# Shift and scale of an adaLN layer by fp32 products with the weight blocks as stationary operand

## The chip, the cores and the metric

The kernel runs on one core of a Trainium2 chip. TensorE (PE) multiplies, VectorE (DVE), ScalarE (ACT) and GpSimd (POOL) do the element-wise work, SyncE (SP) issues most DMAs. The metric is the device time of one execution in microseconds (us), as the median of several runs. A trace of one execution, taken by the hardware profiler, gives the times of single instructions; "PEld" in it is TensorE's weight load, which is recorded apart from the matmul.

## The reference

One layer of a hybrid decoder: a prompt of 4096 tokens and eight sample tokens, with 1024 features. What matters here is its beginning:

```python
mod = (c @ w_ada + b_ada)[:, None, :]          # c: (1, 1024) and (8, 1024), w_ada: (1024, 3072)
shift, scale, gate = jnp.split(mod, 3, axis=-1)
h = x * (1 + scale) + shift
proj = h @ w_in
...
y = layer_norm(DEEPNORM_ALPHA * x + (1 + gate) * mix, ln_g, ln_b)
```

`c` has nine rows in all, one for the prompt and eight for the samples. Nothing of the projection can start before shift and scale are there. Everything behind `proj` (a gated delta rule in chunks with a recurrent state, sliding-window attention, output projection, normalisation) is the same before and after the change.

## The kernel before

The kernel keeps features on the partitions: `shiftT`, `scaleT` and `gateT` are tiles of 128 partitions x 8 blocks x 9 rows of `c`. Phase 1 (`body`, up to line 736) runs over 16 stretches of 256 tokens: `xt` scales and shifts x into `hT`, an fp16 high part and an fp16 low part, and `front` multiplies it by 12 weight blocks `w1` of 128 columns, each split into fp16 high and low parts, with 24 products of 256 columns per block (`group`, line 307), beside 32 small products for `bd` (lines 265 and 267). Then come the recurrent parts of the stretch (`gdn_inv`, `gdn_c`) and side work: `gate_cols` and `dec_a` in the first stretches, preparation of later weights (`prep`, `prep_s`). Phases 2 and 3 follow with attention, the z gates and the output.

The stage that the change touches lies ahead of all this. w_ada's first 2048 columns are read in 16 pieces of 512 KB (`ada`, line 147: 128 rows of 1024 columns, in the order of the rows), each into one of six buffers that `raw` hands out in turn (three names, two buffers each). ACT casts a piece to fp16 (`split`, line 178), DVE forms the low part (line 179), and PE multiplies the pieces as moving operand, 512 columns at a time, with the 18 columns of `cT16` (c's high and low part) as stationary operand (line 190). The results are rows: they are copied out of PSUM (lines 195 and 197), turned by 16 fp32 products with two stacked identities (line 200), and b_ada is added (`shiftT` line 201, `scaleT` line 202).

Right behind it, `xt(0, xs, True)` (line 700) forms hT of the first stretch in four pairs of blocks: ACT and DVE scale and shift one block each (lines 253 and 250), ACT casts the pair (line 255), DVE forms the low part (line 256). `hs32` and `hsT` are the same for the samples (lines 206 to 209). The w1 blocks are fetched through the same six buffers (`fetch_w1`, line 216) and split by ACT and DVE (`split_w1`), first blocks 4 to 7, then the others.

`gate_cols` (line 164), which runs one block for each stretch as side work, already uses the other form: blocks of w_ada as stationary fp32 operand, `cT` as moving operand of 9 columns (line 173).

A scheduler orders the instructions of each engine when the program is built; on the chip every engine, and SP's queue of DMAs, works through its own list in order. A buffer is written again only when its readers are done, and dependencies are kept by the region of a tile that an instruction touches (PE reads the high part of hT's first pair before the others are written).

Of the kernel before, what the change touches and what calls it, by code (L numbers as in the profile page):

```python
# [9 lines left out]
F32 = mybir.dt.float32  # L10
F16 = mybir.dt.float16
BF16 = mybir.dt.bfloat16
AF = mybir.ActivationFunctionType
ALU = mybir.AluOpType
# [9 lines left out]
IWS = 1.0 / WS  # L24
# [9 lines left out]
def body(ctx, tc, I, O, seq):  # L34
# [3 lines left out]
    pe, act, dve, pool, sp = nc.tensor, nc.scalar, nc.vector, nc.gpsimd, nc.sync  # L38

    def mm(out, l, r, st=True, sp_=True):  # L40
        pe.matmul(out, l, r, start=st, stop=sp_)  # L41
# [5 lines left out]
    cf = cst.tile([128, 713], F32, name="cf")  # L47
# [25 lines left out]
    shiftT = cst.tile([128, 8, 9], F32, name="shiftT")  # L73
    scaleT = cst.tile([128, 8, 9], F32, name="scaleT")
    gateT = cst.tile([128, 8, 9], F32, name="gateT")
    cols = cst.tile([128, 73], F32, name="cols")
# [34 lines left out]
    with ExitStack() as p1:  # L111
# [3 lines left out]
        w1p = p1.enter_context(tc.tile_pool(name="w1p", bufs=1))  # L115
        stg = p1.enter_context(tc.tile_pool(name="stg", bufs=2))
        wk = p1.enter_context(tc.tile_pool(name="wk", bufs=2))
        sml = p1.enter_context(tc.tile_pool(name="sml", bufs=2))
        pga = p1.enter_context(tc.tile_pool(name="pga", bufs=1, space=PSUM))
# [3 lines left out]
        pgi = p1.enter_context(tc.tile_pool(name="pgi", bufs=3, space=PSUM))  # L123
# [4 lines left out]
        def xt_ps(shape, dt=F32):  # L128
            return pxt.tile(shape, dt, name="xt")

        def load_x(s):

            xs = []
            for q in range(2):
                x = wf.tile([128, 4, 256], F32, name="x", bufs=3)
                sp.dma_start(x, I["xT"][s][:, 4 * q:4 * q + 4])
                xs.append(x)
            return xs
# [3 lines left out]
        def raw():  # L142

            nraw[0] += 1
            return wk.tile([128, 1024], F32, name=("Aqk", "Kd", "Vn")[nraw[0] % 3], bufs=2)

        def ada(i):
            st = raw()
            sp.dma_start(st, I["w_ada"][0, i // 2 * 128:i // 2 * 128 + 128, i % 2 * 1024:i % 2 * 1024 + 1024])
            return st  # L150

        adas = [ada(i) for i in range(6)]
        cT = w1p.tile([128, 8, 9], F32, name="cT")
        act.dma_start(cT, I["cT"])
        act.dma_start(cols, I["cols"])
        hs32 = w1p.tile([128, 8, 8], F32, name="hs32")
        act.dma_start(hs32, I["xsT"])
        xs = load_x(0)
        cT16 = w1p.tile([128, 8, 18], F16, name="cT16")
        dve.tensor_copy(cT16[:, :, 0:9], cT)  # L160
        dve.tensor_sub(cT16[:, :, 9:18], cT, cT16[:, :, 0:9])
        dve.tensor_scalar(cw64, cols[:, 60:72], IWS, None, op0=ALU.mult)

        def gate_cols():
            part, dst, one = 2, gateT, 1.0
            for blk in range(8):
                cc = part * 8 + blk
                ps = xt_ps([128, 9])
                for hf in range(2):
                    st = stg.tile([128, 4, 256], F32, name="stg")[:, 0:2].rearrange("p a (b c) -> p (a b) c", c=128)  # L170
                    sp.dma_start(st, I["wg"][blk][:, 4 * hf:4 * hf + 4])
                    for k in range(4):
                        mm(ps, st[:, k, :], cT[:, 4 * hf + k, :], hf + k == 0, hf + k == 4)
                dve.tensor_scalar(dst[:, blk, :], ps, cols[:, cc:cc + 1], one, op0=ALU.add, op1=ALU.add)
                yield

        def split(dst_h, dst_l, src):
            act.activation(dst_h, src, AF.Copy, scale=WS)
            dve.scalar_tensor_tensor(dst_l, src, WS, dst_h, op0=ALU.mult, op1=ALU.subtract)


        rps = [pgi.tile([18, 512], F32, name="pgi") for _ in range(3)] + [pga.tile([18, 512], F32, name="pga")]
        for k in range(8):
            w16 = wk.tile([128, 2, 2, 1024], F16, name="kqv", bufs=2)
            for z in range(2):
                st = adas[2 * k + z] if 2 * k + z < 6 else ada(2 * k + z)
                split(w16[:, z, 0], w16[:, z, 1], st)
                for wi, m in ((0, 18), (1, 9)):
                    for q in range(2):
                        mm(rps[2 * z + q][0:m], cT16[:, k, 0:m], w16[:, z, wi, q * 512:(q + 1) * 512],  # L190
                           k + wi == 0, k == 7 and wi == 1)
        arow = wk.tile([18, 2048], F32, name="kqv", bufs=2)
        for q in range(4):
            if q % 2 == 0:
                act.activation(arow[:, q * 512:(q + 1) * 512], rps[q], AF.Copy, scale=IWS)
            else:
                dve.tensor_scalar(arow[:, q * 512:(q + 1) * 512], rps[q], IWS, None, op0=ALU.mult)
        ps = pgi.tile([128, 16, 9], F32, name="pgi")
        for b in range(16):
            mm(ps[:, b, :], arow[:, b * 128:(b + 1) * 128], cf[0:18, 704:713])  # L200
        dve.tensor_add(shiftT, ps[:, 0:8, :], cols[:, 0:8, None].to_broadcast([128, 8, 9]))
        dve.scalar_tensor_tensor(scaleT, ps[:, 8:16, :], 1.0, cols[:, 8:16, None].to_broadcast([128, 8, 9]),
                                 op0=ALU.add, op1=ALU.add)


        dve.tensor_mul(hs32, hs32, scaleT[:, :, 1:9])
# [497 lines left out]
        for g in (0, 1, 2, 3, 8, 9, 10, 11):  # L704
            split_w1(g, fetch_w1(g))
        npre = npres = 0
        sides = [gate_cols(), dec_a()]

        def ahead(s):
            if s < NS:  # L710
                nxt[0] = xt(s, load_x(s))

        for s in range(NS):
            kqv, G, sc, U16, Aqk, Kd, Vn, eGl, vt, vt16 = front(s, nxt[0], lambda: ahead(s + 1))
# [25 lines left out]
    with ExitStack() as p2:  # L740
# [11 lines left out]
        wa = p2a.enter_context(tc.tile_pool(name="wa", bufs=2, **W2))  # L752
        wk = p2a.enter_context(tc.tile_pool(name="wk2", bufs=2, **W2))
# [400 lines left out]
        def mixes(s):  # L1154

            z = zq.pop(s)
            m = []
            for t, (oa, ob) in enumerate(oq_.pop(s)):
                for h in range(4):
                    hs = slice(h * 128, (h + 1) * 128)  # L1160
                    dve.scalar_tensor_tensor(oa[:, hs], oa[:, hs], fS[:, 2 * s + t, h:h + 1], z[t, 0][:, hs],
                                             op0=ALU.mult, op1=ALU.mult)
                dve.tensor_mul(ob, ob, z[t, 1].rearrange("p (a j d) -> p j a d", a=2, j=4))
                m.append((oa, ob.rearrange("p j a d -> p (j a d)")))
            return m
# [162 lines left out]
        m = mixes(0)  # L1328
# [5 lines left out]
        for s in range(NS):  # L1334
# [13 lines left out]
            if ahead:  # L1348
                m = mixes(s + 1)
# [47 lines left out]
def layouts(a):  # L1397

    seq = a["x_prompt"].shape[1]
    ns = seq // 256  # L1400
    w_in, w_out, w_ada = a["w_in"][0], a["w_out"][0], a["w_ada"][0]

    def cols(w, n):

        return w.reshape(-1, 128, n, 128).transpose(2, 1, 0, 3)

    def chan(v):

        return v.reshape(v.shape[0], -1, 128).transpose(2, 1, 0)

    wz = np.stack([cols(w_in[:, c0:c0 + 512], 4) for c0 in (OFF_AZ, OFF_BZ)])
    wz = wz.reshape(2, 4, 128, 2, 2, 2, 128).transpose(1, 4, 2, 3, 0, 5, 6)
    wa = w_out[0:512].reshape(2, 2, 128, 2, 4, 128).transpose(4, 0, 2, 3, 1, 5)
    wb = w_out[512:].reshape(2, 2, 2, 64, 2, 4, 128).transpose(5, 1, 0, 3, 4, 2, 6)
    ws = np.stack([wz.reshape(8, 128, 4, 256),
                   np.concatenate([wa.reshape(8, 128, 2, 256), wb.reshape(8, 128, 2, 256)], 2)])
    rows = np.concatenate([w_out[0:512].reshape(4, 128, 1024),
                           w_out[512:].reshape(2, 4, 64, 1024).transpose(1, 0, 2, 3).reshape(4, 128, 1024)])
    out = {
        "xT": a["x_prompt"][0].reshape(ns, 256, 8, 128).transpose(0, 3, 2, 1),  # L1420
        "xsT": chan(a["x_sample"][:, 0]),
        "cT": chan(np.concatenate([a["c_prompt"], a["c_sample"]])),
        "cols": np.concatenate([a["b_ada"][0].reshape(24, 128), a["conv_w"][0].reshape(48, 128), a["norm_a"]]).T,
        "w1": cols(w_in[:, 0:1536], 12),
        "wbd": w_in[:, OFF_BD:OFF_BD + 8].reshape(8, 128, 8).transpose(1, 0, 2),
        "wb": cols(w_in[:, OFF_BQ:OFF_BZ], 6),
        "ws": ws,
        "wg": cols(w_ada[:, 2048:], 8),
        "wdec": rows.reshape(8, 128, 8, 128).transpose(2, 1, 0, 3),
        "scT": a["state_conv"][0].reshape(8, 3, 12, 128).transpose(3, 2, 0, 1),  # L1430
        "ckT": a["cache_swa_k"][0].reshape(8, 128, 128).transpose(2, 0, 1),
        "cvT": a["cache_swa_v"][0].reshape(8, 128, 128).transpose(1, 0, 2),
        "sink64": np.tile(a["sinks"].reshape(8, 1), (8, 1)),
    }
    return {k: np.ascontiguousarray(v) for k, v in out.items()}
# [25 lines left out]
```

## Time and profile before

| | |
|---|---|
| time, median of 3 runs | 2232.67 us (2229.04 to 2239.25) |
| time of the profiled execution | 2235.6 us |
| its span, first to last instruction | 2233.5 us |
| mean granted TensorE clock | 0.985 of full speed |
| PE busy | 2094.1 us, 94% |
| DVE busy | 1830.9 us, 82% |
| ACT busy | 1268.2 us, 57% |
| chain that ended last | PE 54%, DVE 29%, ACT 10%, waits for DMA 3% |

The span runs from the first instruction to the last; the 2.1 us between it and the execution's time lie around the program. "Busy" is the time in which an engine had an instruction in work; matmuls are pipelined and one has a length of 0.2 to 0.6 us, so PE can be busy without a gap and still not be at its peak. The granted clock is what the chip gave TensorE, as a share of 2.4 GHz; it has two levels, 1.00 and 0.50. The chain that ended last is followed back from the last instruction, at each step to what released it.

### The profile page before, as it was taken

The numbers are of one execution on the slowest core, as the hardware profiler recorded it, in microseconds if no ns is written. First come the engines' busy times: TensorE is split into PE (matmuls) and PEld (weight loads), VectorE is DVE, ScalarE is ACT, GpSimd is POOL, SyncE is SP. The second block draws the span as 40 slices with busy tenths as digits, with TensorE's granted clock in tenths as the row PEclk, the third lists the DMA queues.
The fourth block names the chain that finished last, engine by engine and source line by source line (L and its number), as shares of the span: only waits on it lengthen the run. The fifth ranks groups of instructions, "written<-read, shape, count | busy, mean of one in ns | idle before, by whom it ended". The sixth has DMA issues, their size and how long they took to land.

```text
span 2233.5 us, 48871 instructions
## 1 busy us (share of the span) xinstructions
PE 2094.1 (94%) x18287; PEld 1493.4 (67%) x18287; DVE 1830.9 (82%) x5539; ACT 1268.2 (57%) x3601; POOL 161.7 (7%) x284
## 2 busy tenths in 40 slices
PE   6989999999899999998999999999999999999997
PEld 3868888888788888776677677776455445444443
DVE  7778889888889989888878877777686787888877
ACT  6766877677667776665456666666442333334332
POOL 1111111101111111011000000000000000000000
PEclk9999999999999999999999999999998999999999
DMA  8333322332323332213163111110532333323231
GB/s 326 112 119 96 124 87 92 119 105 82 91 83 106 106 115 81 72 51 119 44 239 112 44 58 65 56 58 23 222 113 89 119 114 114 117 87 132 95 100 71
DMA packets 140733, 232.19 MB, mean 104 GB/s; under 512 B 62804, under 2 KB 74376, under 8 KB 134328
## 3 DMA queue, kind: packets, MB, share of 16 engines
q1 hardware_dynamic: 139200, 228.53, 30.6%
q8 instruction: 143, 2.34, 0.4%
q14 instruction: 94, 0.77, 0.1%
q10 hardware_dynamic: 1296, 0.55, 0.1%
HBM read 154.07 MB, written 76.09 MB: 103 GB/s over the span
## 4 chain that ended last, share of the span: by engine, by line
PE 54%; DVE 29%; ACT 10%; issue 3%; DMA 3%; POOL 0%; SPq 0%; POOLq 0%; ACTq 0%; DVEq 0%
PE pp L1041 21%; PE pj L41 11%; PE pgi L41 7%; DVE kqv L315 6%; DVE lt L421 3%; PE pga L41 3%; ACT Sm L872 3%; DVE LV L423 3%; PE po L41 2%; PE tr L889 2%; PE tr L41 2%; PE xt L41 1%; DVE kqv L322 1%; DVE Sm L865 1%; PE pS L41 1%
## 5 line engine op out<-in xcount | busy, mean ns | idle before, releaser
L41 PE MATMUL pj<-hT,w 128*128 128x256 f16 x4608 | 572.1, 274 | 3.4 <-ACT hT L255 2.6
L41 PEld LDWEIGHTS <-w 128*128 128x128 f16 x4800 | 448.1, 98 | 63.5 <-issue 11.5
L1041 PEld LDWEIGHTS <-S 128*128 128x128 f16 x1536 | 150.9, 99 | 172.2 <-issue 6.4
L41 PEld LDWEIGHTS <-hT 128*128 128x128 f16 x2048 | 159.5, 98 | 69.6 <-issue 4.8
L41 PE MATMUL pj<-wq,hT 128*128 128x512 f16 x768 | 197.6, 379 | 0.8 <-ACT v L816 0.5
L1041 PE MATMUL pp<-wz,S 128*128 128x512 f16 x768 | 183.6, 386 | 0.0
L315 DVE SCALAR_TENSOR_TENSOR kqv<-u,cols,kqv 128x256 f32<-128x256 f32 x384 | 180.8, 477 | 1.9 <-ACT kqv L313 1.4
L1041 PE MATMUL pp<-wo,S 128*128 128x512 f16 x768 | 171.5, 379 | 0.7 <-DVE zs L1217 0.6
L872 ACT ACTIVATE Sm<-Sm,nm 128x256 f32<-128x256 f32 (+1 forms) x256 | 125.4, 492 | 40.1 <-DVE nm L869 40.0
L1041 PE MATMUL pp<-wz,hT 128*128 128x512 f16 x576 | 131.6, 379 | 1.2 <-ACT zs L1128 1.2
L421 DVE TENSOR_TENSOR lt<-LV,LU 128x60 f32<-128x60 f32 (+24 forms) x496 | 119.2, 240 | 5.8
L1041 PE MATMUL pp<-wo,A 128*128 128x512 f16 x540 | 122.9, 380 | 0.0
L865 DVE CUSTOM_DVE_ANT_0 Sm<-pS,swam 128x256 f32<-128x256 f32 (+1 forms) x256 | 96.0, 414 | 24.4 <-PE tr L889 23.6
L1041 PEld LDWEIGHTS <-hT 128*128 128x128 f16 x612 | 59.6, 98 | 71.8 <-issue 2.6
L41 PE MATMUL pj<-wkv,hT 128*128 128x256 f16 x768 | 105.4, 273 | 2.2 <-DVE qt L783 1.4
L423 DVE TENSOR_TENSOR LV<-LV,lt 128x60 f32<-128x60 f32 (+24 forms) x496 | 102.5, 207 | 5.8
L1080 POOL TENSOR_TENSOR rs<-rs,cf 128x1 f32<-128x1 f32 (+1 forms) x33 | 22.4, 680 | 1073.5 <-DVE rs L1079 1073.5
L41 PE MATMUL pga<-kqv 128*128 128x256 f32 x256 | 72.1, 400 | 25.0 <-DVE kqv L322 24.9
L1041 PEld LDWEIGHTS <-A 128*128 128x128 f16 x540 | 53.1, 99 | 62.8 <-issue 1.4
L1022 ACT ACTIVATE S<-zt 128x512 f16<-128x512 f32 x64 | 40.1, 631 | 87.3 <-DVE zt L1028 82.6
L1135 ACT ACTIVATE zs<-zs 128x512 f32<-128x512 f32 x48 | 30.2, 629 | 98.0 <-DVE zs L1134 98.0
L889 PE MATMUL tr<-cf,Sm 128*128 128x128 f32 x504 | 83.6, 284 | 0.8
(378 smaller groups left out, 4561.5 us busy)
## 6 DMA issues: line engine op xcount, KB each, us to landing
hT<-hD SPq DMA_DIRECT2D x32, 1024.0 KB, 4.8
x<-in_xT_dram SPq DMA_DIRECT2D x32, 512.0 KB, 5.4
hD<-hT SPq DMA_DIRECT2D x16, 1024.0 KB, 4.3
x<-in_x_prompt_dram SPq DMA_DIRECT2D x60, 256.0 KB, 3.3
out_y_prompt_dram<-x SPq DMA_DIRECT2D x60, 256.0 KB, 2.1
stg<-in_ws_dram SPq DMA_DIRECT2D x16, 512.0 KB, 4.0
LU<-D SPq DMA_DIRECT2D x64, 128.0 KB, 3.5
wS<-wt SPq DMA_DIRECT2D x16, 512.0 KB
```

What stands on the lines that cost most here:

```text
L41: pe.matmul(out, l, r, start=st, stop=sp_)
L315: dve.scalar_tensor_tensor(d, u[:, b2, j:j + 256], cwj(j, blk), d, op0=ALU.mult, op1=ALU.add)
L322: dve.scalar_tensor_tensor(dst, th, 1.0, dst, op0=ALU.add, op1=ALU.mult)
L421: dve.tensor_mul(lt[:, j0:, 0:j], LV[:, j0:, j:j + 1].to_broadcast([128, n, j]), LU[:, None, 0:j, j].to_broadcast([128, n, j]))
L423: dve.tensor_add(LV[:, j0:, 0:j], LV[:, j0:, 0:j], lt[:, j0:, 0:j])
L865: dve.tensor_tensor_reduce(Sm[:, h, k0:256], pS[:, h2, k0:256], swam[:, k0:256], 0.125, -1e30, op0=ALU.add, op1=ALU.max, accum_out=mx[:, h ...
L872: act.activation(Sm[:, h, k0:256], Sm[:, h, k0:256], AF.Exp, bias=nm[:, h:h + 1], accum_out=sm_[:, h:h + 1])
L889: pe.transpose(pt[:, h2, kb, :], Sm[:, h + h2, kb * 128:(kb + 1) * 128], ident)
L1022: act.activation(q[:, 0], src, AF.Copy)
L1041: pe.matmul(dst.rearrange("p (u c) -> p u c", c=128), A[:, hi, k, :], W[:, k // 2::2, q, wi, k % 2, :], start=new and n == 0, stop=n == 11 ...
L1080: pool.tensor_tensor(rs[0:n, 1:2], rs[0:n, 0:1], half_neg[0:n, 0:1], op=ALU.pow)
L1135: act.activation(zs, zs, AF.Silu, scale=IWS)
```

## The change

w_ada's pieces become blocks of 128 columns: `wa` holds for each of 24 blocks the 128 partitions x 8 row blocks x 128 columns (512 KB, contiguous for each partition). The first 16 blocks (8 for shift, 8 for scale) are read in the order shift 0, scale 0, shift 1, scale 1 and so on, through the same buffers. Each block takes part in 8 fp32 products as stationary operand, with `cT[:, k]` of 9 columns as moving operand, which add up in PSUM and give shift or scale by channel. Blocks 0 to 3 of both form the first half, blocks 4 to 7 the second; behind each half b_ada is added into the half of `shiftT` and `scaleT`. The fp16 copies, `cT16`, the row results and their turning are gone. `gate_cols` reads its blocks from `wa`, and w_ada itself is no input of the program any more.

```diff
-        def ada(i):
-            st = raw()
-            sp.dma_start(st, I["w_ada"][0, i // 2 * 128:i // 2 * 128 + 128, i % 2 * 1024:i % 2 * 1024 + 1024])
+        def ada(blk):
+
+            st = raw().rearrange("p (k c) -> p k c", k=8)
+            sp.dma_start(st, I["wa"][blk])
             return st
 
-        adas = [ada(i) for i in range(6)]
+        order = [8 * z + k for k in range(8) for z in range(2)]
+        adas = [ada(b) for b in order[:6]]
...
-        cT16 = w1p.tile([128, 8, 18], F16, name="cT16")
-        dve.tensor_copy(cT16[:, :, 0:9], cT)
-        dve.tensor_sub(cT16[:, :, 9:18], cT, cT16[:, :, 0:9])
...
-                    sp.dma_start(st, I["wg"][blk][:, 4 * hf:4 * hf + 4])
+                    sp.dma_start(st, I["wa"][cc][:, 4 * hf:4 * hf + 4])
...
-        rps = [pgi.tile([18, 512], F32, name="pgi") for _ in range(3)] + [pga.tile([18, 512], F32, name="pga")]
-        for k in range(8):
-            w16 = wk.tile([128, 2, 2, 1024], F16, name="kqv", bufs=2)
-            for z in range(2):
-                st = adas[2 * k + z] if 2 * k + z < 6 else ada(2 * k + z)
-                split(w16[:, z, 0], w16[:, z, 1], st)
-                for wi, m in ((0, 18), (1, 9)):
-                    for q in range(2):
-                        mm(rps[2 * z + q][0:m], cT16[:, k, 0:m], w16[:, z, wi, q * 512:(q + 1) * 512],
-                           k + wi == 0, k == 7 and wi == 1)
-        arow = wk.tile([18, 2048], F32, name="kqv", bufs=2)
-        for q in range(4):
-            if q % 2 == 0:
-                act.activation(arow[:, q * 512:(q + 1) * 512], rps[q], AF.Copy, scale=IWS)
-            else:
-                dve.tensor_scalar(arow[:, q * 512:(q + 1) * 512], rps[q], IWS, None, op0=ALU.mult)
-        ps = pgi.tile([128, 16, 9], F32, name="pgi")
-        for b in range(16):
-            mm(ps[:, b, :], arow[:, b * 128:(b + 1) * 128], cf[0:18, 704:713])
-        dve.tensor_add(shiftT, ps[:, 0:8, :], cols[:, 0:8, None].to_broadcast([128, 8, 9]))
-        dve.scalar_tensor_tensor(scaleT, ps[:, 8:16, :], 1.0, cols[:, 8:16, None].to_broadcast([128, 8, 9]),
-                                 op0=ALU.add, op1=ALU.add)
+        for half in range(2):
+            ps = pgi.tile([128, 4, 2, 9], F32, name="pgi")
+            for i in range(8 * half, 8 * half + 8):
+                st = adas[i] if i < 6 else ada(order[i])
+                for k in range(8):
+                    mm(ps[:, i // 2 % 4, i % 2, :], st[:, k, :], cT[:, k, :], k == 0, k == 7)
+            c0, c1 = 4 * half, 4 * half + 4
+            dve.tensor_add(shiftT[:, c0:c1], ps[:, :, 0, :], cols[:, c0:c1, None].to_broadcast([128, 4, 9]))
+            dve.scalar_tensor_tensor(scaleT[:, c0:c1], ps[:, :, 1, :], 1.0,
+                                     cols[:, 8 + c0:8 + c1, None].to_broadcast([128, 4, 9]), op0=ALU.add, op1=ALU.add)
...
-        "wg": cols(w_ada[:, 2048:], 8),
+        "wa": cols(w_ada, 24),
```

## Rows read from the trace of the kernel before

**Rows 1.** Busy time by stretch: stretch, length, busy us (instructions) by engine, PEclk, DMA.

```profile
18.50:32.20 13.70, 11.35 (x47) 4.02 (x46) 12.48 (x12) 10.94 (x11) 0.00 (x0) 1.00 1.02 392
...
40.40:45.80 5.40, 4.70 (x50) 3.31 (x50) 5.40 (x11) 5.40 (x10) 0.00 (x0) 0.50 0.40 109
45.80:60.00 14.20, 14.20 (x137) 12.73 (x134) 14.20 (x33) 11.40 (x21) 2.91 (x3) 1.00 0.96 381
```

**Rows 2.** In order of time, the start: start us, length, engine, line, what.

```profile
10.68 0.20 DVE L160 CAST cT<-cT 128x72 f16<-128x72 f32 x1 [3.50 <-DMA cT<-in_cT_dram]
...
15.46 0.63 PE L41 MATMUL pga<-kqv,cT 128*18 128x512 f16 x1
15.89 0.63 PE L41 MATMUL pgi<-kqv,cT 128*9 128x512 f16 x1
...
18.90 0.38 PE L41 MATMUL pgi<-kqv,cT 128*9 128x512 f16 x1
19.12 0.38 PE L41 MATMUL pga<-kqv,cT 128*9 128x512 f16 x1
```

**Rows 3.** In order of time, PE's first projection products.

```profile
40.47 0.59 PE L41 MATMUL pj<-hT,w 128*128 128x256 f16 x2 [2.62 <-ACT hT L255]
...
45.27 0.67 PE L41 MATMUL tr<-wbd,hT 128*128 128x8 f16 x18
45.80 15.66 PE L41 MATMUL pj<-hT,w 128*128 128x256 f16 x142
62.38 0.17 PE L41 MATMUL tr<-g,c 128*128 128x8 f16 x1 [0.92 <-DVE g L283]
```

**Rows 4.** The gate's fp32 products: all (busy, mean ns), two runs of weight loads.

```profile
L41 PE MATMUL xt<-cT,stg 128*128 128x9 f32 x128 | 15.0, 252 | 0.0
...
176.09 0.97 PEld L41 LDWEIGHTS xt<-cT,stg 128*128 128x128 f32 x8
...
534.76 1.86 PEld L41 LDWEIGHTS xt<-cT,stg 128*128 128x128 f32 x16
```

**Rows 5.** In order of time, fp32 weight loads for the products with S.

```profile
170.63 1.60 PEld L41 LDWEIGHTS pgi<-S,kqv 128*128 128x128 f32 x7
...
170.63 1.81 PEld L41 LDWEIGHTS pgi<-S,kqv 128*128 128x128 f32 x8
...
179.82 1.87 PEld L41 LDWEIGHTS pgi<-S,kqv 128*128 128x128 f32 x16
```

**Rows 6.** Busy time by stretch, later: rows 5's two places, narrow and wide products.

```profile
170.70:172.40 1.70, 1.70 (x10) 1.70 (x9) 1.64 (x4) 0.91 (x1) 0.00 (x0) 0.50 0.04 10
...
179.90:181.60 1.70, 1.70 (x16) 1.70 (x16) 1.60 (x8) 0.98 (x7) 0.00 (x0) 1.00 1.08 250
...
1670.90:1673.90 3.00, 3.00 (x108) 2.95 (x107) 2.57 (x5) 2.06 (x4) 0.83 (x1) 1.00 0.73 228
1674.00:1677.30 3.30, 3.30 (x77) 3.30 (x75) 3.03 (x6) 0.78 (x2) 0.00 (x0) 0.50 0.51 188
...
1684.20:1687.60 3.40, 3.40 (x17) 1.57 (x16) 1.89 (x5) 0.95 (x2) 0.00 (x0) 1.00 0.00 0
```

**Rows 7.** In order of time, a run of narrow products on PE.

```profile
1670.93 9.98 PE L41 MATMUL tr<-hsT,wz 128*128 128x16 f16 x256
```

**Rows 8.** In order of time, SP's queue: the first load of w1.

```profile
26.41 0.33 SPq L216 DMA_DIRECT2D Vn<-in_w_dram  x1
```

**Rows 9.** In order of time, around shift; then groups by line (busy, mean ns).

```profile
36.17 1.04 ACT L178 ACTIVATE w<-Kd 128x1024 f16<-128x1024 f32 x1
...
37.72 0.23 DVE L201 TENSOR_TENSOR shiftT<-pgi,cols 128x72 f32<-128x72 f32 x1 [0.96 <-PE pgi L41]
...
38.13 1.09 ACT L253 ACTIVATE x<-x,shiftT,scaleT 128x256 f32<-128x256 f32 x2 [0.92 <-DVE scaleT L202]
...
L255 ACT ACTIVATE hT<-x 128x512 f16<-128x512 f32 x6 | 3.5, 617 | 0.1
...
L179 DVE SCALAR_TENSOR_TENSOR w<-Kd,w 128x1024 f16<-128x1024 f32 x4 | 4.9, 1217 | 0.0
```

More of the change, by code (lines that the diff above doesn't have):

```diff
@@ L1447 @@
     arrays.update(layouts(arrays))
-    for k in ("w_in", "w_out", "c_prompt", "c_sample", "b_ada", "conv_w", "norm_a"):
+    for k in ("w_in", "w_out", "c_prompt", "c_sample", "w_ada", "b_ada", "conv_w", "norm_a"):
         del arrays[k]
```

## The prediction

> **What bounds the kernel now.** I read the page first: TensorE (PE) is busy for 94% of the span and heads the chain that ended last, so whatever delays PE's first useful product is not given back easily, unless another engine paces the stretch behind it. The change touches one place only, the 38 us before the first projection; so the views to read are the busy time by stretch, then the instructions in order around that stage, then the price of the one new operation.
>
> The stretches [rows 1] show the old stage and what follows. From 18.5 to 32.2 us the pace is DVE's: 12 of its instructions, nearly all fp16 low parts, fill 12.48 of 13.70 us, while ACT and PE have gaps. From 40.4 to 45.8 PE works with a granted clock of 0.50, the lower of its two levels (1.2 and 2.4 GHz). From 45.8 on PE is full at 2.4 GHz, and DVE is full at the same time. In order of time [rows 3, 9]: shift is formed at 37.72, PE starts its first projection product at 40.47 after 2.62 us without work, issues 17 of them (2, 6 and 9, between other work) and the 32 small products for `bd` up to 45.80, and then runs 142 projection products in 15.66 us without a gap. The next wait of PE is 0.92 us for DVE at 62.38. So what counts is when PE may begin the projections, and how soon after that it runs at 2.4 GHz.
>
> The clock column needs care at the very start: it shows 1.00 from the first microsecond, before PE has done anything, yet two neighbouring 512-column products start 0.43 us apart at 15.46 and 15.89, and 0.22 us apart at 18.90 and 19.12 [rows 2]. So PE begins this kernel at 1.2 GHz and reaches 2.4 only near 18.5 us, after several microseconds of 512-column products.
>
> **The change part by part.**
>
> Removed: 16 ACT casts and 16 DVE low parts of w_ada, 64 fp16 products of 512 columns, four copies of the row results, 16 fp32 products against the two stacked identities, the two cT16 instructions. All of it lies ahead of 37.7 us, so its worth is exactly what the new stage doesn't take again.
>
> Added: 16 blocks x 8 = 128 fp32 products with a 128x128 stationary block and 9 moving columns. The trace has this very form, from the gate: 64 such products (8 blocks of 8) stand as 128 records, so each product is two weight loads and two matmuls [rows 4]. The new stage is therefore 256 such pairs. At the gate eight weight loads took 0.97 us and sixteen 1.86, so each further one adds 0.111 us, (1.86 - 0.97) / 8. This is at 2.4 GHz; 256 x 0.111 = 28.5 us is the lower end.
>
> The upper end comes from the same weight loads at 1.2 GHz. The fp32 loads of `kqv` blocks for the products with S take 1.87 us for 16 where the granted clock is 1.00, the same pace as the gate's, although they move 128 columns; where it is 0.50, seven take 1.60 us and eight 1.81, so 0.21 us each [rows 5, 6]. So at 2.4 GHz it is the weight load that paces both, and at 1.2 GHz its pace is half. 256 x 0.211 = 54.0 us; twice the gate's own pace would make 57.
>
> Which of the two? The rows that come nearest are a run of 256 products with 16 or 8 columns, back to back for 9.98 us from 1670.93 [rows 7]. PE and its weight loads are busy 3.30 of 3.30 us in it, and yet the clock that had been 1.00 is 0.50 at 1674.0; it is 1.00 again at 1684.2, after the 512-column products have come back [rows 6]. So a PE that is full of narrow products falls to 1.2 GHz and does not climb out of it. The new stage starts at 1.2 GHz, since PE has done nothing before it, and holds nothing but 9-column products: the next work for PE needs w1, whose loads stand behind the 16 loads of w_ada in SP's queue [rows 8]. I take the price at 1.2 GHz for all of it, 54.0 us.
>
> The Trainium skill (TensorE: Matmul & The Clock Gate, "Why this matters for your kernels") says that a TensorE kept busy without a break gets to its full clock. By that rule the stage would take 28.5 us; the trace disagrees where the columns are few, as above. It is the first rival below.
>
> Start: PE needs cT and the first block; DVE's first use of cT, released by its load, is at 10.68 [rows 2], and blocks have landed by then. So the stage runs from 10.7 to 64.7, a product's own 0.25 us is left [rows 4], and shift is formed at 65.0 instead of 37.72 [rows 9]: **27.3 us later**. DMA doesn't pace it: a block of 512 KB every 3.4 us is well under what the queue does now. The same 16 loads of the same size stand on SP; only what frees their six buffers moves, from DVE's low part to PE's eighth product. Behind them on SP: the first w1 load goes out at 26.41 now [rows 8], and then waits for block 11, 10.7 + 11 x 3.4 = 48; the next three follow at 3.4 us each. The w1 loads, the store of hT and the next x all wait in that queue, which costs nothing as long as they land before 64.7; four or five w1 blocks do.
>
> Moved: x's blocks 0 to 3 of hT are formed after the first half, near 38 us, with ACT and DVE idle. When the second half is done PE can go straight on with the products for k = 0 to 3 (12 in each w1 block) while ACT and DVE form k = 4 to 7. Now it waits from 37.7 to 40.47 and again behind that.
>
> What is given back depends on one thing that this trace can't show: where the w1 splits stand in ACT's queue, which is in order. Now three splits run ahead of the first ACT instruction that needs scale (the third at 36.17, that instruction at 38.13) [rows 9]. If they are ahead again, PE starts at 64.7 and does what it had done by 45.80, 17 products at 0.21 us (256 columns, half of the 0.43 us that 512 take at 1.2 GHz [rows 2]) and 1.2 us for `bd` (18 of its 32 took 0.67) [rows 3], by 69.5: **+23.7**. If they stand behind the second half of x, ACT first has two scalings of 0.55 us and two casts of 0.62, then one split of 1.04 [rows 9]; from 65.0 + 0.4 that is 68.8, and PE is level at 73.6: **+27.8**. PE then climbs to 2.4 GHz some 5 us after it has begun, as now (40.47 to 45.8), so the clock behind the stage costs the same. I see no row that decides the order and take the middle, **+26**. Behind this point PE is full, so little returns; the 0.92 us wait for DVE may.
>
> Edits at nothing: gate blocks read from `wa` are the same 256 KB pieces; w_ada is no longer an input. The two cT16 instructions are DVE's while it waits anyway.
>
> Sum: the profiled execution took 2235.6 us (span 2233.5), 2.9 above the median of the three runs, inside their spread. 2235.6 + 26 = 2261.6; against the median, 2232.7 + 26 = **2259**. Bounds: +22 (first order, and the waits behind return 2) to +31 (second order, 57 us in place of 54): 2255 to 2264. The places where the clock dips later can shift by one or two dips of 3.4 us at half speed, 1.7 us each: 2251 to 2267.
>
> **The rivals.**
> 1. *The stage runs at the price of 2.4 GHz*, because the clock does rise in it, or because the load's pace doesn't follow the clock with only 9 columns behind it. For: at the gate the form did run at 1.00, among other work. Against: PE and its weight loads were just as full from 1670.93 on [rows 6, 7]. Stage end 10.7 + 28.5 + 0.25 = 39.5, shift 1.8 us later than now; but PE goes on at once and has never dropped, so 17 products at 0.11, `bd` and the wait for k = 4 (some 41) put it level near 42.5 instead of 45.8: -3.3, **2229**, not slower than before. It decides from the pace: below about (37.7 + 5 - 10.95) / 256 = 0.124 us for each pair the change breaks even.
> 2. *DVE is what paces 38 to 62 us*: it is full there [rows 1]. Then what leaves its queue behind the shift returns in full: three splits of 1.22 [rows 9] and the first half of x (two scalings of 0.4, two low parts of 0.7), 5.9 us, and the wait at 62.38: 27.3 - 6.8 = +20.5, **2253**. Against: PE shows no gap from 45.8 to 61.5.
> 3. *The halves bring nothing*: ACT's first scaling waits for both halves of scaleT, and the splits stand behind all of x. Then 65.4 + 4.7 of ACT + 1.0 = 71.1, PE level at 75.9, +30; with the dearer products +33, **2266**.
>
> **How the numbers follow.** Forecast (+22 to +31) 0.62; rival 1 0.12; rival 2 0.11; rival 3 0.12; 0.03 for orders further on that I can't see. The range leaves out rival 1 and the tails: 2248 to 2268. A measurement of this kernel tells about 0.5%, 11 us, from no change. Only rival 1 and part of the unseen lie below +11: within 0.5% 0.10, faster 0.04, slower 0.86.
>
> **What would show it.** Right: products of `pgi` from `cT` with a stationary f32 block, 256 records, 0.21 us from start to start, from 10.7 to about 65; granted clock 0.50 from where its record begins in the stage to a few us behind it; DVE and ACT almost idle from 12 to 60; shift's second half at 65; PE's first projection product at 65 (order one) or 69 (order two), full speed near 70 to 75. Wrong: 16 records in under 2 us inside the stage (rival 1), PE gaps behind 70 us that DVE ends (rival 2), no hT instruction before 60 us (rival 3).

## The result, and the profile after

The changed kernel takes 2259.44 us (median of 4 runs, 2258.31 to 2261.03), the kernel before beside it 2233.57 us (2229.04 to 2239.25): a ratio of 1.011, 95% interval 1.0095 to 1.0126, so 25.9 us slower. The profiled execution took 2258.91 us, with a span of 2257.0. The forecast was 2259, between 2248 and 2268.

The page of the changed kernel, first part: engine, busy us, share of the span, instructions.

```profile
span 2257.0 us, 49133 instructions
...
PE 2126.0 (94%) x18447; PEld 1538.4 (68%) x18447; DVE 1809.9 (80%) x5521; ACT 1251.7 (55%) x3583; POOL 168.8 (7%) x284
```

PE is busy 31.9 us longer than before, DVE 21.0 and ACT 16.5 us less. The shares hardly moved: the page alone would not tell that the kernel has become slower by taking work off two engines and giving it to the third.

The changed kernel in order of time, from the first product of the new stage to the next wait of PE behind it (start us, length, engine, line, what). The lines of the code behind the stage are 13 lower than before.

```profile
10.99 3.58 PE L41 MATMUL pgi<-cT,Kd 128*128 128x9 f32 x16 [3.44 <-DMA cT<-in_cT_dram]
...
14.36 3.53 PEld L41 LDWEIGHTS pgi<-cT,Vn 128*128 128x128 f32 x16
14.43 3.56 PE L41 MATMUL pgi<-cT,Vn 128*128 128x9 f32 x16
...
38.50 0.20 DVE L188 TENSOR_TENSOR shiftT<-pgi,cols 128x36 f32<-128x36 f32 x1 [24.93 <-PE pgi L41]
38.84 1.09 ACT L240 ACTIVATE x<-x,shiftT,scaleT 128x256 f32<-128x256 f32 x2 [29.49 <-DVE scaleT L189]
...
48.74 0.33 SPq L203 DMA_DIRECT2D Vn<-in_w_dram  x1
...
62.21 3.56 PE L41 MATMUL pgi<-cT,Kd 128*128 128x9 f32 x16
...
65.81 0.20 DVE L188 TENSOR_TENSOR shiftT<-pgi,cols 128x36 f32<-128x36 f32 x1 [24.04 <-PE pgi L41]
66.14 1.09 ACT L240 ACTIVATE x<-x,shiftT,scaleT 128x256 f32<-128x256 f32 x2 [25.18 <-DVE scaleT L189]
...
67.14 1.13 ACT L242 ACTIVATE hT<-x 128x512 f16<-128x512 f32 x2
...
68.18 1.04 ACT L177 ACTIVATE w<-Vn 128x1024 f16<-128x1024 f32 x1
...
69.27 0.61 PE L41 MATMUL pj<-hT,w 128*128 128x256 f16 x2 [3.50 <-ACT w L177]
70.53 6.48 PE L41 MATMUL pj<-hT,w 128*128 128x256 f16 x39 [0.65 <-DVE w L178]
76.85 0.95 PE L41 MATMUL tr<-wbd,hT 128*128 128x16 f16 x32
77.67 14.35 PE L41 MATMUL pj<-hT,w 128*128 128x256 f16 x130
93.61 0.18 PE L41 MATMUL tr<-g,c 128*128 128x8 f16 x1 [1.59 <-DVE g L270]
```

Read it from the top. Sixteen blocks, 16 records each, follow one another from 10.99 to 62.21: (62.21 - 10.99) / 15 = 3.41 us a block, 0.213 us for each load and matmul. That is the pace of the fp32 loads at a granted clock of 0.50 [rows 5, 6], not that of the gate [rows 4]. The first half's shift stands at 38.50, about where all of shift stood before (37.72) [rows 9]; the second half's stands at 65.81. Then the order of ACT's queue shows: two scalings from 66.14, two casts from 67.14, and only then, at 68.18, the first split of a w1 block, though its load had been issued at 48.74 (26.41 before) [rows 8]. PE has waited 3.50 us for that split and starts the projections at 69.27 in place of 40.47 [rows 3].

Busy time by stretch of the changed kernel (stretch, length, busy us and instructions of PE, PEld, DVE, ACT, POOL, granted clock, DMA share, GB/s).

```profile
10.90:38.00 27.10, 27.01 (x127) 27.01 (x127) 0.24 (x2) 0.00 (x0) 0.00 (x0) 1.00 0.65 220
38.00:65.00 27.00, 27.00 (x129) 27.00 (x128) 2.33 (x6) 2.13 (x4) 0.00 (x0) 1.00 0.42 138
65.90:69.20 3.30, 0.00 (x0) 0.00 (x0) 2.83 (x10) 3.06 (x6) 0.00 (x0) 1.00 0.00 0
74.80:88.00 13.20, 13.20 (x147) 11.91 (x146) 9.05 (x22) 9.63 (x17) 1.60 (x2) 1.00 0.88 311
```

For 54 us PE and its weight loads have no gap, while DVE and ACT do almost nothing; from 65.9 to 69.2 it is the other way round. Behind 74.8 PE is full, DVE has 9.05 of 13.20 us: it was full in the same work before [rows 1]. The clock column must not be believed in the first three rows. In this execution its record begins with a rise at 74.8 us, and the column shows 1.00 for all that lies ahead of it, as at the start of the kernel before [rows 2]. The spacing of 0.213 us is what tells the clock here; the run with products ahead of the stage, further down, has the clock on record.

### The profile page after: what moved, and what is told of

Read it like the earlier page. It is cut to its first block, busy times and chain, and to the rows that moved or that the text cites. A ratio compares the mean times of both kernels' runs of the same rounds, so it can differ in the third digit from the quotient of the medians.

```text
span 2257.0 us, 49133 instructions
## 1 busy us (share of the span) xinstructions
PE 2126.0 (94%) x18447; PEld 1538.4 (68%) x18447; DVE 1809.9 (80%) x5521; ACT 1251.7 (55%) x3583; POOL 168.8 (7%) x284
## 4 chain that ended last, share of the span: by engine, by line
PE 56%; DVE 28%; ACT 10%; issue 3%; DMA 2%; POOL 0%; SPq 0%; POOLq 0%; ACTq 0%; DVEq 0%
PE pp L1028 21%; PE pj L41 12%; PE pgi L41 9%; DVE kqv L302 5%; DVE lt L408 3%; PE pga L41 3%; ACT Sm L859 3%; DVE LV L410 2%; PE po L41 2%; PE tr L876 2%; PE tr L41 2%; DVE Sm L852 1%; DVE kqv L309 1%; PE xt L41 1%; PE pS L41 1%
## 5 line engine op out<-in xcount | busy, mean ns | idle before, releaser
L852 DVE CUSTOM_DVE_ANT_0 Sm<-pS,swam 128x256 f32<-128x256 f32 (+1 forms) x256 | 96.0, 414 | 24.4 <-PE tr L876 23.7
L240 ACT ACTIVATE x<-x,shiftT,scaleT 128x256 f32<-128x256 f32 x124 | 67.6, 606 | 60.0 <-DVE scaleT L189 54.7
```

Of the source, the lines that this page charges most:

```text
L240: act.activation(h32[:, kk], h32[:, kk], AF.Identity, bias=shiftT[:, k, 0:1], scale=scaleT[:, k, 0:1])
L852: dve.tensor_tensor_reduce(Sm[:, h, k0:256], pS[:, h2, k0:256], swam[:, k0:256], 0.125, -1e30, op0=ALU.add, op1=ALU.max, accum_out=mx[:, h ...
```

## The experiments

The theory: each of the 256 pairs costs 0.213 us because the stage starts at 1.2 GHz and its own products never bring the clock up; what the stage takes, the kernel loses. The rivals: another cause for 0.213 us than the clock; a stage that hides behind DVE's work further on; a loss at the seam (order of splits, halves) rather than in the stage. All edits are to the changed kernel. The kernel before ran beside each.

| kernel | ratio to before | 95% interval |
|---|---|---|
| changed | 1.0110 | 1.0095 to 1.0126 |
| changed, again | 1.0112 | 1.0096 to 1.0128 |
| 126 columns | 1.0010 | 0.9996 to 1.0024 |
| 63 columns | 1.0127 | 1.0109 to 1.0145 |
| 9 columns, products ahead of the stage | 1.0102 | 1.0089 to 1.0115 |
| half of the contraction | 1.0007 | 0.9993 to 1.0021 |
| one piece in place of halves | 1.0113 | 1.0095 to 1.0132 |
| four w1 blocks early | 1.0117 | 1.0095 to 1.0139 |
| the same, and `bd`'s weights early | 1.0111 | 1.0095 to 1.0127 |
| all: ahead, 126 columns, early | 1.0012 | 1.0001 to 1.0022 |

**126 columns.** The same blocks and the same number of loads, but `cT[:, k]` is read 14 times over as moving operand, and shift and scale are taken from the first copy, in quarters. It makes the matmuls dearer; forming shift and scale in quarters also changes the order of work at the end of the stage.

```diff
-            ps = pgi.tile([128, 4, 2, 9], F32, name="pgi")
+            for qt in range(2):
+                ps = pgi.tile([128, 2, 2, 14, 9], F32, name="pgi")
...
-                    mm(ps[:, i // 2 % 4, i % 2, :], st[:, k, :], cT[:, k, :], k == 0, k == 7)
+                        mm(ps[:, i // 2 % 2, i % 2], st[:, k, :], cT[:, k, None, :].to_broadcast([128, 14, 9]),
+                           k == 0, k == 7)
```

> The changed kernel with 126 moving columns in place of 9 (cT read 14 times over; only the first nine results are used), added up in quarters of PSUM. The same 256 weight loads. Theory (the stage is paced by fp32 weight loads at 1.2 GHz, because nothing but 9-column products stands on TensorE): the clock rises some microseconds into the stage, the distance of the loads falls from 0.21 to 0.11 us, the stage ends near 43 to 46 us instead of 65.7, time about 2238 us. Rival (0.21 us is what a load of this form takes here, whatever the clock): stage end 65 us or later, time 2259 us or above.

Measured: 2237.96 us, before 2236.28. In order of time, PE and, at the end of the stage, ACT:

```profile
10.82 3.58 PE L41 MATMUL pgi<-cT,Kd 128*128 128x126 f32 x16 [3.46 <-DMA cT<-in_cT_dram]
14.24 1.95 PE L41 MATMUL pgi<-cT,Vn 128*128 128x126 f32 x16
...
36.66 1.06 ACT L177 ACTIVATE w<-Vn 128x1024 f16<-128x1024 f32 x1 [1.01 <-DMA Vn<-in_w_dram]
...
39.25 1.95 PE L41 MATMUL pgi<-cT,Kd 128*128 128x126 f32 x16
...
40.51 1.06 ACT L177 ACTIVATE w<-Aqk 128x1024 f16<-128x1024 f32 x1 [2.79 <-DMA Aqk<-in_w_dram]
41.04 2.49 PE L41 MATMUL pj<-hT,w 128*128 128x256 f16 x20
...
41.53 0.60 ACT L243 ACTIVATE x<-x,shiftT,scaleT 128x256 f32<-128x256 f32 x1
...
44.05 0.27 PE L41 MATMUL pj<-hT,w 128*128 128x256 f16 x1 [0.53 <-ACT hT L245]
44.61 1.08 PE L41 MATMUL pj<-hT,w 128*128 128x256 f16 x8 [0.28 <-DVE w L178]
```

The first block takes 3.4 us from start to start, as before the edit, and the clock's record has a rise at 14.07 us. From there 14 blocks take (39.25 - 14.24) / 14 = 1.79 us each, 0.112 us a load. The pace changes inside the first quarter, so it isn't the quarters that change it: the price of 0.213 us was the clock's, and not that of the form or of the loads. Fourteen times the columns make the stage 24 us shorter, and the loss is gone. Not all of that is the stage's, though. Two w1 splits ran at 36.66 and 40.51, ahead of the last scaling at 41.53, so PE went on at 41.04 without the wait of 3.50 us; its first projection product comes 28.2 us earlier than in the changed kernel (69.27 - 41.04). What the other order is worth in the time, this run doesn't tell.

**63 columns.** Half of that, in the halves of the changed kernel.

```diff
-                    mm(ps[:, i // 2 % 4, i % 2, :], st[:, k, :], cT[:, k, :], k == 0, k == 7)
+                    mm(ps[:, i // 2 % 4, i % 2], st[:, k, :], cT[:, k, None, :].to_broadcast([128, 7, 9]),
+                       k == 0, k == 7)
```

> As the run with 126 columns, but 63 (cT read 7 times). Theory: there are two levels and nothing between them, so either the clock rises and the time is about 2238 us, or it stays at 0.50 in the whole stage and the time is 2259 us; which one isn't known beforehand. Rival (the pace depends on the columns themselves and not on the clock): a distance between loads between 0.11 and 0.21 us and a time in between, about 2248 us.

Measured: 2262.86 us. In order of time:

```profile
14.37 3.62 PE L41 MATMUL pgi<-cT,Vn 128*128 128x63 f32 x16
...
62.16 3.62 PE L41 MATMUL pgi<-cT,Kd 128*128 128x63 f32 x16
69.28 0.61 PE L41 MATMUL pj<-hT,w 128*128 128x256 f16 x2 [3.50 <-ACT w L177]
```

With 63 columns the stage is that of 9 columns to 0.05 us: (62.16 - 14.37) / 14 = 3.41 us a block, first projection at 69.28. The broadcast operand of the kernel with 126 columns is therefore not what helped; in these kernels only two paces occur, and nothing between.

**Products ahead of the stage.** 24 fp16 products of 512 columns on a zeroed tile, whose result nobody uses, run while PE would wait for the first loads; the stage itself has 9 columns again.

```diff
+        XE = w1p.tile([128, 2, 4, 128], F16, name="XE")
+        dve.memset(XE, 0.0)
+        pw = tr_ps([128, 512])
+        xw = XE.rearrange("p a h c -> p (a h c)")
+        for _ in range(24):
+            mm(pw, XE[:, 0, 0, :], xw[:, 0:512])
...
```

> The changed kernel with 24 products of 512 columns on zeroed data put ahead of the stage, so that TensorE enters it at 2.4 GHz; the stage keeps its 9 columns. Theory (narrow products let the clock fall): the first blocks go at 0.11 us for a load, the clock is at 0.50 again within a few us, the stage ends 2 to 4 us earlier than 65.7 and the time is 2255 to 2258 us. Rival (only the cold start keeps the clock low, and a stage that starts warm stays warm): stage end near 40 us, time about 2232 us.

Measured: 2260.41 us. First in order of time, then by stretch:

```profile
1.45 6.64 PE L41 MATMUL tr<-XE 128*128 128x512 f16 x24 [1.45 <-DVE hist L226]
10.62 3.32 PE L41 MATMUL pgi<-cT,Kd 128*128 128x9 f32 x16 [2.52 <-DMA cT<-in_cT_dram]
13.79 3.56 PE L41 MATMUL pgi<-cT,Vn 128*128 128x9 f32 x16
```

```profile
4.20:8.00 3.80, 3.80 (x18) 1.57 (x16) 0.66 (x3) 0.34 (x1) 0.00 (x0) 1.00 0.69 217
11.00:25.00 14.00, 14.00 (x69) 14.00 (x68) 0.25 (x2) 0.00 (x0) 0.00 (x0) 0.50 0.76 279
45.00:65.00 20.00, 20.00 (x95) 20.00 (x95) 0.00 (x0) 0.00 (x0) 0.00 (x0) 0.50 0.40 132
```

Here the record begins early, so the column can be read: 1.00 in and behind the products ahead, 0.50 through the stage, with PE and its loads busy in every microsecond of it. The fall is recorded at 10.94 us, 0.3 us into the stage, so of the first blocks at 0.11 us a load that were expected only two or three loads came: the first block takes 13.79 - 10.62 = 3.17 us in place of 3.41. PE had waited 2.52 us for cT in between, so this run doesn't show whether a stage that follows at once would have kept the clock for longer. It shows that the stage doesn't bring it back.

**Half of the contraction.** Only k = 0 to 3 are multiplied; the kernel leaves out half of the sum in shift and scale. All loads stay.

```diff
-                for k in range(8):
-                    mm(ps[:, i // 2 % 4, i % 2, :], st[:, k, :], cT[:, k, :], k == 0, k == 7)
+                for k in range(4):
+                    mm(ps[:, i // 2 % 4, i % 2, :], st[:, k, :], cT[:, k, :], k == 0, k == 3)
```

> The changed kernel with the products of k = 0 to 3 alone, so that shift and scale come from half of the contraction: 64 products, 128 weight loads, all 16 blocks still read. Theory: the length of the stage goes to the end of the kernel one for one, 128 x 0.213 = 27.3 us less: shift's second half near 38.5, time about 2232 us. Rival (another engine paces what lies behind, so that part of it doesn't show): 20 us less or fewer, 2239 us or above.

Measured: 2237.02 us, before 2236.28. In order of time:

```profile
12.60 1.85 PE L41 MATMUL pgi<-cT,Vn 128*128 128x9 f32 x8
14.31 1.85 PE L41 MATMUL pgi<-cT,Aqk 128*128 128x9 f32 x8
...
38.39 0.20 DVE L188 TENSOR_TENSOR shiftT<-pgi,cols 128x36 f32<-128x36 f32 x1 [10.38 <-PE pgi L41]
41.85 0.61 PE L41 MATMUL pj<-hT,w 128*128 128x256 f16 x2 [3.50 <-ACT w L177]
```

The pace is the same (8 records from 12.60 to 14.31, 0.214 us each), the stage half as long, and DMA keeps up with twice the rate of blocks. The first projection comes 27.4 us earlier than in the changed kernel (69.27 - 41.85), and the kernel gets back 0.0103 x 2236 = 23 us; with the two intervals, 5 us to either side. The stage lies on the path nearly one for one. That all of it comes back fits, and that some 4 us don't fits as well: the theory's number (27.3 us less, 2232) is missed by about that much, and this run doesn't tell why. Against the kernel before it stands 1.4 us later at the first projection (41.85 and 40.47) and 0.0007 x 2236 = 1.6 us in the time; so the few us that don't add up seem to be the changed kernel's own, which is 28.8 us late at that point and 25.9 in the time.

**One piece.** One PSUM tile, shift and scale formed once, behind all 16 blocks.

```diff
-        for half in range(2):
-            ps = pgi.tile([128, 4, 2, 9], F32, name="pgi")
-            for i in range(8 * half, 8 * half + 8):
+        ps = pgi.tile([128, 8, 2, 9], F32, name="pgi")
+        for i in range(16):
...
+        dve.tensor_add(shiftT, ps[:, :, 0, :], cols[:, 0:8, None].to_broadcast([128, 8, 9]))
```

> The changed kernel with shift and scale formed once, behind all 16 blocks, in place of two halves. Theory (the halves take half of the first x off the path behind the stage): ACT has four scalings and four casts ahead of the first split in place of two and two, so TensorE's first projection product comes 2.2 to 2.6 us later, near 71.6, and the time is 2261 to 2263 us. Rival (the splits, DVE or the clock decide, not x): first product at the same instant within 0.5 us.

Measured: 2262.06 us, before 2237.51. In order of time:

```profile
65.45 0.23 DVE L186 TENSOR_TENSOR shiftT<-pgi,cols 128x72 f32<-128x72 f32 x1 [51.96 <-PE pgi L41]
...
71.02 0.61 PE L41 MATMUL pj<-hT,w 128*128 128x256 f16 x2 [5.60 <-ACT w L177]
```

From shift to the first projection it now takes 5.57 us, with halves 3.46 (65.81 to 69.27). So the halves are worth 2.1 us at this point: ACT has two scalings and two casts fewer between the stage and the first split. In the time, 1.0113 against 1.0110, nothing of it can be seen.

**Four w1 blocks early.** Loads of w1 blocks 4 to 7 stand between the first four blocks of w_ada, and their splits ahead of everything that needs scale; x's work then ends the wait.

```diff
-        adas = [ada(b) for b in order[:6]]
...
+        adas, wst = [], []
+        for n in range(4):
+            adas.append(ada(order[n]))
+            wst.append(fetch_w1(4 + n))
+            split_w1(4 + n, wst[n])
...
```

> The changed kernel with w1's blocks 4 to 7 read and split between the first four blocks of w_ada, so that these four splits stand ahead of x in ACT's queue. Theory: TensorE no longer waits from 65.7 to 69.3 us for a split; it has projection products at hand at the latest when the stage ends, so 3.6 to 6 us less, 2253 to 2256 us. Rival (the wait is covered by what TensorE or DVE have to do later anyway): 2259 us.

Measured: 2259.82 us. In order of time:

```profile
45.08 2.72 PE L41 MATMUL pj<-hT,w 128*128 128x256 f16 x12
...
71.48 0.59 PE L41 MATMUL tr<-wbd,hT 128*128 128x16 f16 x6 [1.67 <-DVE wbd L156]
```

The gain of 3.6 to 6 us that the theory promised isn't there. With w1 at hand, projection products were placed into the second half of the stage (24 of them), and PE waited for `bd`'s weights at the end. I took that wait for what had replaced the other, and tried it:

**`bd`'s weights early as well.**

```diff
+            if n == 0:
+                load_bd()
...
         nxt = [xt(0, xs, True)]
-        load_bd()
```

> As the run with the w1 splits early, and the small weights of bd loaded and split early too, since their products stood at the head of TensorE's list and waited for them to 71.5 us. Theory (behind the stage TensorE is the bound, and this wait took the place of the one for the splits): the gain that did not show then shows now, 2252 to 2256 us. Rival (DVE or the clock paces the first stretch, whatever TensorE finds at hand): 2259 us as without it.

Measured: 2262.07 us, no gain again. In order of time:

```profile
43.93 2.72 PE L41 MATMUL pj<-hT,w 128*128 128x256 f16 x12
46.45 3.42 PE L41 MATMUL pgi<-cT,Aqk 128*128 128x9 f32 x16
...
68.70 0.20 DVE L213 TENSOR_TENSOR shiftT<-pgi,cols 128x36 f32<-128x36 f32 x1 [28.70 <-PE pgi L41]
...
70.70 0.22 PE L41 MATMUL tr<-wbd,hT 128*128 128x16 f16 x2 [2.04 <-ACT hT L248]
```

The theory of the replaced wait falls. Twelve products from 43.93 to 46.45 are 0.21 us each: what was brought forward ran at 1.2 GHz, and shift's second half came at 68.70 in place of 65.81. The clock's rise came at 75.3 us, 71.6 in the second execution of the changed kernel, which ran beside it. At the 49th projection product the two kernels are level, 26.8 and 27.0 us behind the kernel before. Here the work moved into the stage, which was full on PE, was no work saved.

**All together.** The products ahead, 126 columns, w1 and `bd`'s weights early; the edits are those shown.

> All that helped together: 24 products of 512 columns ahead of the stage, 126 moving columns, w1 blocks 4 to 7 and bd's weights early. Theory: the stage runs at 0.112 us a load from its start, 10.8 + 28.7 us and the 1.1 us of projection products among it, shift's second half near 41 us, TensorE full at 2.4 GHz from there, level with before 3 to 5 us earlier than in before; time 2229 to 2234 us, 0.1 to 0.3% faster than before at best. Rival (DVE, full between 38 and 62 us in before, or the first stretch's longer time at 1.2 GHz takes it back): 2236 us or above.

Measured: 2239.26 us, ratio 1.0012. In order of time:

```profile
8.92 1.95 PE L41 MATMUL pgi<-cT,Kd 128*128 128x126 f32 x16
...
16.35 2.05 PE L41 MATMUL pgi<-cT,Kd 128*128 128x126 f32 x16 [0.86 <-DMA Kd<-in_wa_dram]
21.04 0.21 PE L41 MATMUL tr<-wbd,hT 128*128 128x16 f16 x2 [2.64 <-ACT hT L257]
...
42.47 1.95 PE L41 MATMUL pgi<-cT,Vn 128*128 128x126 f32 x16
```

The first block is fast at once (1.95 us), but the stage's last block stands at 42.47, later than with 126 columns alone (39.25). At the higher pace PE waits for the loads of w_ada (0.86 us, and 0.69 once more), which now share the queue with w1, and for hT (2.64 us), because its own queue is in order. The 2229 to 2234 us that were expected didn't come. Put together like this, with the stage at 2.4 GHz throughout, the form is not faster than the kernel before; it is level. An order in which w1's loads don't delay those of w_ada was not tried.

**The two kernels again.** The changed kernel a second time, and one more look at the kernel before.

> The changed kernel once more, unaltered, beside the next three on the same chip, with a second profile. Theory (the late part of the kernel, where the first profile of before lost some 7 us against that of the changed kernel, differs by chance from execution to execution): first projection product again at 69.3 us, time about 2259 us, but the instants in the last third may stand some us later or earlier than in the first profile. Rival (the change itself speeds the late part): the same instants again within 1 us.

> The kernel before, unaltered, for a second profile. Theory (what the first profile of before lost between 1700 and 1830 us against every other profile is chance): against the first profile the same instants up to 1700 us within 1 to 3 us, and a different loss behind. Rival (it belongs to the kernel): the same instants within 1 us to the end.

```profile
67.88 0.61 PE L41 MATMUL pj<-hT,w 128*128 128x256 f16 x2 [3.50 <-ACT w L177]
```

That is the changed kernel again, in order of time: first projection 27.4 us later than [rows 3]. Its span is 2261.8 us; the kernel before has one of 2228.0 in its second execution. In the first pair of profiles the changed kernel is 28.8 us behind at the first projection, 29.2 at the 49th, 32.4 at the 864th, and only 23.5 at the end. In the second pair it is 28.4, 28.0, 31.0 and 33.8 at the same places, so the ends of two single executions tell the loss to some 5 us at best. The last fall in the first pair lies between 1700 and 1830 us, where the first execution of the kernel before lost 5 us that its second one didn't lose: its granted clock was 0.50 from 1728.7 to 1732.0 and from 1769.6 to 1772.8, that of the second execution 1.00 in both. So nothing is given back there; it was chance in one execution.

## Why the prediction was right, step by step

- **The price of a pair.** Forecast 0.211 us, measured 0.213; 256 pairs take 54.6 us, forecast 54.0. The step that carried the prediction was the choice between the two ends, 28.5 and 54.0 us, by the run of narrow products that fell to 0.50 and stayed there [rows 6, 7]. The kernels with 63 and 126 columns, and the one with products ahead, show the choice to be the clock's. The Trainium skill (TensorE: Matmul & The Clock Gate, "Why this matters for your kernels") would have a TensorE that is kept busy get to its full clock; here it was busy for 54 us without a gap and did not. The Trainium skill (TensorE: Matmul & The Clock Gate, "LDWEIGHTS (loading the stationary operand)") gives a load's ns as its columns divided by 1.2, without a clock; worked out for 128 columns that is an estimate of 107 ns. The trace is near it at 2.4 GHz (0.112 us) and not at 1.2 (0.213).
- **Start and end.** Forecast 10.7 to 64.7 with shift at 65.0; seen 10.99 to some 65.6 with shift at 65.81. DMA did not pace it, and the first w1 load went out at 48.74 (48). The granted clock was back at 74.8 (70 to 75).
- **The order on ACT.** This is where I chose nothing: +23.7 if the splits ran ahead, +27.8 behind, and the middle, +26, for want of a row. The second order came, with PE's first product at 69.27 (68.8). By its own mechanism the forecast should then have been +28, and at the first projection products the changed kernel is 28.8 and 27.4 us behind. The sum also let PE run on from there, but PE waited once more, 0.65 us at 70.53, for DVE's low part of the split, which has no term in it; at the 49th product the kernel is 29.2 us behind. The medians say +25.9 and +24.9, and +26.6 for 63 columns, whose stage and order are the same. The four spans say 28.7 on average, (2257.0 + 2261.8 - 2233.5 - 2228.0) / 2, but that leans on one execution: the second one of the kernel before took 2230.1 us, and the median of the runs beside it is 2237.5. So the middle hit the medians more closely than either order that could happen. That is luck and not a merit of the sum: runs of the kernel before lie between 2229 and 2244 us, and terms of 2 to 4 us are not resolved in the time.
- **Rival 1**, the price of 2.4 GHz, did not happen. The kernel with 126 columns, though formed in quarters, comes nearest to what it would have been: level, +1.7 us to the kernel beside it (2237.96 and 2236.28) where the rival had -3.3. The first block ran at 1.2 GHz, the stage ended at 41.0 in place of 39.5, and PE waited for ACT and DVE behind it (0.53 and 0.28 us). That is 2.3 of the 5 us; the other 2.7 lie inside the interval, 3 us to either side, and are not explained.
- **Rival 2**, DVE as the pace from 38 to 62 us, falls in its strong form: DVE has room now, 9.05 of 13.20 us, and PE runs 130 products without a gap where it ran 142; the next wait for DVE is 1.59 us, not shorter than 0.92 [rows 3]. Nor did the kernel with half of the contraction lose much of what its stage gave back, 23 of 27.4 us with 5 to either side.
- **Rival 3**, halves that bring nothing, is half right: the splits do stand behind all of x, but the first half was scaled at 38.84, and that is worth 2.1 us at the first projection.

Open: whether some 3 us of the 28.8 come back in the medians, and where. No comparison resolves it: by the ratios in the table the same three kernels (changed, again, 63 columns) stand 24.6, 25.1 and 28.4 us behind the kernel before, each with some 4 us to either side. The record of the clock behind 80 us doesn't decide it: without the dip that ends each span, it is at 0.50 for 55 and 48 us in the two executions of the kernel before and for 55 and 61 in those of the changed kernel.

## What to carry to other kernels

Price a new stage on TensorE at the clock at which it will run: look for a stretch of the same trace with the same kind of narrow products, see what the granted clock did there, and take the weight load's duration from a row at that clock. Where few columns move (9 and 63 here), the load is the price. Here work was taken off DVE and ACT and given to the engine that bounds the kernel, and that was paid nearly in full: shift is complete 28 us later (65.81 and 37.72), and the kernel is 25.9 us slower. Moving later products into a stage that was full on TensorE gained nothing here, and a few us of queue order behind it were seen in the trace but not in the time.

## What the runs showed of the hardware

- More columns made the same 256 loads faster: 0.213 us each with 9 or 63 columns, 0.112 with 126 from the second block on, at the rise of the granted clock.
- PE and its weight loads were busy from 11 to 65 us without a gap and the granted clock was 0.50, on record in the run with products ahead of the stage (45 to 65 us: 20.00 of 20.00 us busy).
- The fp32 weight load of 128 columns follows TensorE's clock, 0.112 and 0.213 us at its two levels, with the same block to load.
- The clock column of a profile stands at 1.00 ahead of its first record, here for 74.8 us, though the spacing of the loads from 11 to 65 us shows 1.2 GHz.
